# One row of a partition moved from the tail pieces into the first load of a streaming ReLU-mean kernel (127 to 126 rows a partition)

## The chip, the cores and the metric

The kernel runs on one core of a Trainium2 chip. The metric is the device time of one execution in microseconds (us). An execution's span, as the profile draws it, is some 1.3 us shorter than its time.

## The reference

```
batch, seq, dim = 32, 512, 1024
x: float32 [32, 512, 1024]
return mean(maximum(x, 0), axis=-1)      # float32 [32, 512]
```

It is 16,384 rows of 4 KiB, 67.1 MB to be read once, and 64 KiB to be written.

## The kernel before

The rows are dealt to the 128 partitions. The first 128 rows (one block) go one to a partition, in a load of its own; the other 16,256 rows are cut into 128 runs of 127 consecutive rows, one run to a partition. Of these 127, 7 x 16 come in full tiles of 16 rows (8 MiB a load, 64 KiB without a break in each partition) through three buffers, then pieces of 7, 4, 2 and 1 rows, then the last row in column pieces of 512, 256 and 256.

```
    xfirst, xmain = xf[:P, :], xf[P:, :]
    ...
    J = J - 1
    xr = xmain.rearrange("(p j) d -> p j d", p=P, j=J)
    ...
    row_pieces = [7, 4, 2, 1]
    ...
    def buf_free(t):
        if t >= BUFS:
            nc.sync.wait_ge(act, t - BUFS + 1)
            nc.sync.wait_ge(dve, t - BUFS + 1)

    for t in range(full):
        buf_free(t)
        if t == 0:
            load(-1, row0[:, :], xfirst)
        load(t, bufs[t % BUFS][:, :, :], xr[:, t * NB:(t + 1) * NB, :])
        ...                      # (t == BUFS: store of the first block's means)
```

ScalarE (ACT) takes the even rows, with a Relu that accumulates along the row, VectorE (DVE) the odd ones, with max and add. The first block's means stand one to a partition; a 32x32 transpose brings them into four rows of 32, which are stored with four packets. The very last column piece is DVE's; one store of all the other means ends the kernel. The first two loads (the block and tile 0) are issued ahead of the barrier at the kernel's entry.

## Time and profile before

| | before |
|---|---|
| time, median | 161.34 us (161.31 to 161.44, 3 runs) |
| span of the profile | 160.2 us |
| DVE / ACT busy | 46% / 44% |
| packets of the DMA engines, share of 16 engines' span | 97.7% |
| tile 0 computed from / tile 6 from | 22.98 / 139.30 us |

Read it so: with the queue filled nearly all the time and both engines half idle, the time is the time of the transfers, plus what stands ahead of the first packet and what stands behind the last one. A change can matter in three ways only: in how long the bytes take in packets of their size, at the start, and at the end. The lines themselves are in the prediction below.

### The profile page before, as it was taken

The page shows a single profiled execution, that of the slowest core. Times are in us where ns is not written, and L with a number is a line of the kernel's source. Part 1 is how long each engine was busy: PE and PEld are TensorE (multiplying, and loading weights), DVE is VectorE, ACT ScalarE, POOL GpSimd, SP SyncE. Part 2 cuts the span into 40 slices and gives each one's busy share as a digit, 9 for nine tenths or more (in the row PEclk, how much of TensorE's full clock was granted, in tenths as well). Part 3 has the DMA queues.
Part 4 walks back from the last instruction along what each step waited for, and adds up shares of the span by engine and source line. Part 5 has one row for each costly group of instructions (what it writes and reads, how often), then busy time and mean ns, then how long its engine had stood idle before and what let it go on. Part 6 is the DMA issues. An engine that isn't in the chain of part 4 may idle for free. (4 is left out here: it accounts for less than half of the span.)

```text
span 160.2 us, 347 instructions
## 1 busy us (share of the span) xinstructions
DVE 73.3 (46%) x131; ACT 70.4 (44%) x133; POOL 1.3 (1%) x9
## 2 busy tenths in 40 slices
DVE  0000029900498006960079500993009920299984
ACT  1400029800496006950079300991009900299983
POOL 1000000000000000000000000000000000000001
DMA  9969969979989899699699699699699797998992
GB/s 393 507 278 523 507 278 523 442 344 523 409 376 523 360 425 524 294 491 523 262 524 523 262 523 524 262 523 523 262 524 458 327 523 327 425 451 367 419 412 102
DMA packets 2312, 67.18 MB, mean 419 GB/s; under 512 B 392, under 2 KB 648, under 8 KB 1032
## 3 DMA queue, kind: packets, MB, share of 16 engines
q1 hardware_dynamic: 2312, 67.18, 97.7%
HBM read 67.11 MB, written 0.07 MB: 419 GB/s over the span
## 5 line engine op out<-in xcount | busy, mean ns | idle before, releaser
L20 DVE TENSOR_SCALAR_CACHE_REDUCE rows<-rows 128x1024 f32<-128x1024 f32 (+1 forms) x63 | 72.1, 1208 | 78.9 <-DMA rows<-in_x_dram 78.7
L15 ACT ACTIVATE rows<-rows 128x1024 f32<-128x1024 f32 x64 | 66.2, 1035 | 84.1 <-DMA rows<-in_x_dram 83.9
L15 ACT ACTIVATION_READ_ACCUMULATOR rows<-rows 128x1 f32 x64 | 11.9, 186 | 0.0
L20 DVE DVE_READ_ACCUMULATOR rows<-rows 128x1 f32 x63 | 5.2, 82 | 0.0
L168 DVE STREAM_TRANSPOSE turned<-mean 128x32 f32<-128x32 f32 x1 | 0.2, 213 | 5.9 <-ACT row L164 5.9
L164 ACT ACT_TABLE_LOAD x1 | 1.3, 1283 | 3.3 <-DMA row<-in_x_dram 3.3
L157 POOL TENSOR_SCALAR res<-sums 128x112 f32<-128x112 f32 (+1 forms) x2 | 0.5, 250 | 154.0 <-DVE rows L20 154.0
L164 ACT ACTIVATE row<-row 128x1024 f32<-128x1024 f32 x1 | 1.1, 1056 | 0.0
L15 ACT ACTIVATE last<-last 128x512 f32<-128x512 f32 x1 | 0.6, 630 | 0.0
L20 DVE TENSOR_SCALAR_CACHE_REDUCE last<-last 128x256 f32<-128x256 f32 x1 | 0.4, 420 | 0.3 <-DMA last<-in_x_dram 0.3
L197 DVE SCALAR_TENSOR_TENSOR last<-last,scale 128x258 f32<-128x258 f32 x1 | 0.4, 428 | 0.1
L142 POOL MEMSET scale<- 128x258 f32 x1 | 0.3, 314 | 0.0
L187 POOL TENSOR_SCALAR res<-part 128x1 f32<-128x1 f32 x1 | 0.3, 267 | 0.6 <-DVE rows L20 0.6
L164 ACT ACTIVATION_READ_ACCUMULATOR row<-row 128x1 f32 x1 | 0.2, 186 | 0.0
L15 ACT ACTIVATION_READ_ACCUMULATOR last<-last 128x1 f32 x1 | 0.2, 186 | 0.0
L141 POOL MEMSET mean<- 128x32 f32 x1 | 0.1, 126 | 1.5 <-POOLq L55 1.5
L232 POOL MEMSET const-uint8-127<- 128x1 uint8 x1 | 0.1, 103 | 0.0
L232 POOL MEMSET const-bfloat16-1.0<- 128x1 bf16 x1 | 0.1, 102 | 0.0
L232 POOL MEMSET const-float32-0.0<- 128x1 f32 x1 | 0.1, 99 | 0.2 <-issue 0.2
L232 POOL MEMSET const-float32-1.0<- 128x1 f32 x1 | 0.1, 99 | 0.0
L20 DVE DVE_READ_ACCUMULATOR last<-last 128x1 f32 x1 | 0.1, 83 | 0.0
L197 DVE DVE_READ_ACCUMULATOR last<-last,scale 128x1 f32 x1 | 0.1, 82 | 0.0
## 6 DMA issues: line engine op xcount, KB each, us to landing
rows<-in_x_dram SPq DMA_DIRECT2D x1, 3584.0 KB, 38.1
rows<-in_x_dram SPq DMA_DIRECT2D x1, 2048.0 KB, 42.6
rows<-in_x_dram SPq DMA_DIRECT2D x1, 1024.0 KB, 44.7
row<-in_x_dram SPq DMA_DIRECT2D x1, 512.0 KB, 3.3
rows<-in_x_dram SPq DMA_DIRECT2D x1, 512.0 KB, 45.4
last<-in_x_dram SPq DMA_DIRECT2D x1, 256.0 KB, 45.6
last<-in_x_dram SPq DMA_DIRECT2D x2, 128.0 KB, 45.4
rows<-in_x_dram SPq DMA_DIRECT2D x7, 48.8
```

The source lines that it names most:

```text
L15: return nc.scalar.activation(out=src, in_=src, func=ACT.Relu, accum_out=acc)
L20: return nc.vector.tensor_scalar(out=src, in0=src, scalar1=0.0, scalar2=init, op0=ALU.max, op1=ALU.add, accum_out=acc,)
L141: nc.gpsimd.memset(mean0[:, :], 0.0)
L142: nc.gpsimd.memset(scale[:, :], inv).then_inc(pool, 1)
L157: nc.gpsimd.tensor_scalar(out=res[:, lo:hi], in0=sums[:, lo:hi], scalar1=inv, scalar2=0.0, op0=ALU.mult, op1=ALU.add,)
L164: nc.scalar.activation(out=row0[:, :], in_=row0[:, :], func=ACT.Relu, scale=inv, accum_out=mean0[:, 0:1],).then_inc(first, 1)
L168: nc.vector.transpose(turned0[:, :], mean0[:, :]).then_inc(first, 1)
L187: nc.gpsimd.tensor_scalar(out=res[:, J - 2:J - 1], in0=part[:, 0:1], scalar1=part[:, 1:2], scalar2=inv, op0=ALU.add, op1=ALU.mult,).then_i ...
L197: nc.vector.scalar_tensor_tensor(out=last[:, 768:], in0=last[:, 768:], scalar=0.0, in1=scale[:, :], op0=ALU.max, op1=ALU.mult, accum_out=r ...
L232: nc = _bacc.Bacc("TRN2", target_bir_lowering=False, num_devices=1)
```

## The change

126 rows a partition instead of 127. The first two blocks of 128 rows, not only the first, come one row of each to a partition, in one load ahead of the full tiles; in exchange the first tail piece has 6 rows instead of 7. The intent may be read as taking a row from the end of the stream, where computing and loading meet, and giving it to the start, where the computing engines have nothing to do.

```
--- before.py
+++ after.py
@@ -62,9 +62,9 @@
     J = R // P
     inv = 1.0 / D
 
-    xfirst, xmain = xf[:P, :], xf[P:, :]
-    outfirst, outmain = out.flatten()[:P], out.flatten()[P:]
-    J = J - 1
+    xfirst, xmain = xf[:2 * P, :].rearrange("(c p) d -> p c d", c=2), xf[2 * P:, :]
+    outfirst, outmain = out.flatten()[:2 * P], out.flatten()[2 * P:]
+    J = J - 2
     xr = xmain.rearrange("(p j) d -> p j d", p=P, j=J)
     outr = outmain.rearrange("(p j) -> p j", p=P, j=J)
 
@@ -72,7 +72,7 @@
     BUFS = 3
     full = J // NB
 
-    row_pieces = [7, 4, 2, 1]
+    row_pieces = [6, 4, 2, 1]
     assert full * NB + sum(row_pieces) + 1 == J
     col_pieces = [512, 256, 256]
     assert sum(col_pieces) == D
@@ -87,7 +87,7 @@
     last = sbuf("last", P, D + 2)
     scale = sbuf("scale", P, D // 4 + 2)
 
-    row0, mean0, turned0 = sbuf("row0", P, D), sbuf("mean0", P, 32), sbuf("turned0", P, 32)
+    row0, mean0, turned0 = sbuf("row0", P, 2, D), sbuf("mean0", P, 32), sbuf("turned0", P, 32)
 
 
     loaded = [nc.alloc_semaphore(f"loaded{i}") for i in range(full + len(row_pieces) + len(col_pieces) + 1)]
@@ -117,14 +117,15 @@
     for t in range(full):
         buf_free(t)
         if t == 0:
-            load(-1, row0[:, :], xfirst)
+            load(-1, row0[:, :, :], xfirst)
         load(t, bufs[t % BUFS][:, :, :], xr[:, t * NB:(t + 1) * NB, :])
         if t == BUFS:
 
             nc.sync.wait_ge(first, 2)
-            nc.sync.dma_start(
-                out=outfirst.rearrange("(q i) -> q i", i=32), in_=turned0[0:P:32, :],
-            ).then_inc(stored, 16)
+            for c in range(2):
+                nc.sync.dma_start(
+                    out=outfirst[c * P:(c + 1) * P].rearrange("(q i) -> q i", i=32), in_=turned0[c:P:32, :],
+                ).then_inc(stored, 16)
     j0 = full * NB
     buf_free(full)
     xt = bufs[full % BUFS]
@@ -161,9 +162,11 @@
     nc.scalar.wait_ge(pool, 1)
     nc.vector.wait_ge(pool, 1)
     nc.scalar.wait_ge(loaded[-1], 16)
-    nc.scalar.activation(
-        out=row0[:, :], in_=row0[:, :], func=ACT.Relu, scale=inv, accum_out=mean0[:, 0:1],
-    ).then_inc(first, 1)
+    for c in range(2):
+        done = nc.scalar.activation(
+            out=row0[:, c, :], in_=row0[:, c, :], func=ACT.Relu, scale=inv, accum_out=mean0[:, c:c + 1],
+        )
+    done.then_inc(first, 1)
     nc.vector.wait_ge(first, 1)
     nc.vector.transpose(turned0[:, :], mean0[:, :]).then_inc(first, 1)
     for t in range(full):
@@ -207,7 +210,7 @@
     used = [s.num for s in (*loaded, act, dve, pool, first)]
     assert used == list(range(used[0], used[0] + len(used)))
     nc.sync.sem_clear(range(used[0], used[-1] + 1))
-    nc.sync.wait_ge(stored, 32).then_inc(stored, -32)
+    nc.sync.wait_ge(stored, 48).then_inc(stored, -48)
 
     for e, hint in zip(hinted, hints):
         e.br_lt(flag, 1, on_true="rows_begin", on_false="rows_end").branch_hint(hint)
```

More of the change, by code (lines that the diff above doesn't have):

```diff
@@ L63 @@
     inv = 1.0 / D
-    xfirst, xmain = xf[:P, :], xf[P:, :]
-    outfirst, outmain = out.flatten()[:P], out.flatten()[P:]
-    J = J - 1
+    xfirst, xmain = xf[:2 * P, :].rearrange("(c p) d -> p c d", c=2), xf[2 * P:, :]
+    outfirst, outmain = out.flatten()[:2 * P], out.flatten()[2 * P:]
+    J = J - 2
     xr = xmain.rearrange("(p j) d -> p j d", p=P, j=J)
@@ L73 @@
     full = J // NB
-    row_pieces = [7, 4, 2, 1]
+    row_pieces = [6, 4, 2, 1]
     assert full * NB + sum(row_pieces) + 1 == J
@@ L88 @@
     scale = sbuf("scale", P, D // 4 + 2)
-    row0, mean0, turned0 = sbuf("row0", P, D), sbuf("mean0", P, 32), sbuf("turned0", P, 32)
+    row0, mean0, turned0 = sbuf("row0", P, 2, D), sbuf("mean0", P, 32), sbuf("turned0", P, 32)
     loaded = [nc.alloc_semaphore(f"loaded{i}") for i in range(full + len(row_pieces) + len(col_pieces) + 1)]
@@ L119 @@
         if t == 0:
-            load(-1, row0[:, :], xfirst)
+            load(-1, row0[:, :, :], xfirst)
         load(t, bufs[t % BUFS][:, :, :], xr[:, t * NB:(t + 1) * NB, :])
@@ L124 @@
             nc.sync.wait_ge(first, 2)
-            nc.sync.dma_start(
-                out=outfirst.rearrange("(q i) -> q i", i=32), in_=turned0[0:P:32, :],
-            ).then_inc(stored, 16)
+            for c in range(2):
+                nc.sync.dma_start(
+                    out=outfirst[c * P:(c + 1) * P].rearrange("(q i) -> q i", i=32), in_=turned0[c:P:32, :],
+                ).then_inc(stored, 16)
     j0 = full * NB
@@ L163 @@
     nc.scalar.wait_ge(loaded[-1], 16)
-    nc.scalar.activation(
-        out=row0[:, :], in_=row0[:, :], func=ACT.Relu, scale=inv, accum_out=mean0[:, 0:1],
-    ).then_inc(first, 1)
+    for c in range(2):
+        done = nc.scalar.activation(
+            out=row0[:, c, :], in_=row0[:, c, :], func=ACT.Relu, scale=inv, accum_out=mean0[:, c:c + 1],
+        )
+    done.then_inc(first, 1)
     nc.vector.wait_ge(first, 1)
@@ L209 @@
     nc.sync.sem_clear(range(used[0], used[-1] + 1))
-    nc.sync.wait_ge(stored, 32).then_inc(stored, -32)
+    nc.sync.wait_ge(stored, 48).then_inc(stored, -48)
     for e, hint in zip(hinted, hints):
```

## The prediction

> **What bounds the kernel now.** I read the page first, then the waits of the compute engines, the waits of the issuing queue, and last the timeline around the first full tile and around the end. The page gives the balance:
>
> ```profile
> span 160.2 us, 347 instructions
> DVE 73.3 (46%) x131; ACT 70.4 (44%) x133; POOL 1.3 (1%) x9
> ...
> DMA packets 2312, 67.18 MB, mean 419 GB/s; under 512 B 392, under 2 KB 648, under 8 KB 1032
> ...
> q1 hardware_dynamic: 2312, 67.18, 97.7%
> ```
>
> The two computing engines work less than half of the span; the packets fill 97.7% of the time that 16 DMA engines have. So the transfers are the bound. The view of waits says what the engines wait for in the rest of their time, and the waits of the issuing queue say whether the loads are issued early enough:
>
> ```profile
> ACT rows L15 <- DMA rows<-in_x_dram: 83.9, 9, 17.2
> DVE rows L20 <- DMA rows<-in_x_dram: 78.7, 8, 16.9
> ...
> SPq L115 <- DVE rows L20: 104.6, 5, 29.5
> ```
>
> (us in total, times, longest.) ACT and DVE wait for rows alone. The queue waits for DVE to free a buffer, but that wait costs nothing: the page's list of issues has 48.8 us from issue to landing as the median of the full 16-row loads, and one tile takes 19.4 us (next paragraph), so a load stands some two and a half tiles deep in the queue and the 16 engines never run dry.
>
> The timeline gives the rate. Columns are start, duration, engine, line, operation; the bracket is the idle time before:
>
> ```profile
> 22.98 1.22 DVE L20 TENSOR_SCALAR_CACHE_REDUCE rows<-rows 128x1024 f32<-128x1024 f32 x1 [16.86 <-DMA rows<-in_x_dram]
> ...
> 139.30 1.22 DVE L20 TENSOR_SCALAR_CACHE_REDUCE rows<-rows 128x1024 f32<-128x1024 f32 x1 [10.29 <-DMA rows<-in_x_dram]
> ...
> 147.82 1.06 ACT L15 ACTIVATE rows<-rows 128x1024 f32<-128x1024 f32 x1
> 148.42 1.22 DVE L20 TENSOR_SCALAR_CACHE_REDUCE rows<-rows 128x1024 f32<-128x1024 f32 x1
> ...
> 152.71 1.22 DVE L20 TENSOR_SCALAR_CACHE_REDUCE rows<-rows 128x1024 f32<-128x1024 f32 x1 [0.79 <-DMA rows<-in_x_dram]
> ...
> 155.20 1.22 DVE L20 TENSOR_SCALAR_CACHE_REDUCE rows<-rows 128x1024 f32<-128x1024 f32 x1
> ...
> 156.49 0.75 DVE L20 TENSOR_SCALAR_CACHE_REDUCE rows<-rows 128x576 f32<-128x576 f32 x1
> ...
> 157.54 0.42 DVE L20 TENSOR_SCALAR_CACHE_REDUCE last<-last 128x256 f32<-128x256 f32 x1 [0.29 <-DMA last<-in_x_dram]
> ...
> 158.06 0.43 DVE L197 SCALAR_TENSOR_TENSOR last<-last,scale 128x258 f32<-128x258 f32 x1
> ...
> 158.57 0.35 SPq L205 DMA_DIRECT2D out_dram<-res  x1
> ```
>
> Tile 0 of the full tiles has landed at 22.98 and tile 6 at 139.30: six tiles in 116.32 us, 19.39 us for each. That is 8,388,608 bytes in 19.39 us, 432.7 GB/s. The tail pieces then arrive one after the other, each computed nearly as it lands; the last column piece has landed just before 158.06, and the store closes the span 1.6 us after its issue.
>
> **What the Trainium skill says.** "DMA: Bandwidth & Descriptors", section "Where 436 GB/s comes from", gives 16 ports x 32 B x 850 MHz = 435.2 GB/s. The trace agrees: 432.7 GB/s measured is 99.4% of it. So the part of the kernel that decides cannot run noticeably faster in any layout. The same page, section "Latency and other measured facts", has an entry on HBM row pitch at large powers of two: copies with 512 KiB between partitions made 207 GB/s against 214 at full rate, and 4 MiB halved it; adding 4 KiB restored it. The pitch of the kernel before is 127 x 4 KiB = 508 KiB, and no slowing is seen in its trace; that of the change is 126 x 4 KiB = 504 KiB, which no run shows yet. Third, the page's section "Anatomy of one DMA" says that the fixed cost of a load doesn't grow with its size. The trace is in line with it: the first load, 0.5 MB, took 3.3 us to land, of which its packets, as worked out below, fill about 1.8.
>
> **The change part by part.** Every byte is still read once, so only the cost of the bytes by packet size, and their order, changes. The trace's records of single packets have their durations (8 of each load to each of the 16 engines, back to back): 4,096-byte packets take 159 ns, 16,384-byte ones 611, 28,672-byte ones 1,062, 65,536-byte ones 2,418.
>
> - *Added at the front:* one more row to each partition in the first load, 8 more 4 KiB packets per engine: 8 x 0.159 = 1.27 us. As a check, the single-row piece at the end took 156.49 - 155.20 = 1.29 us. Those packets stand in the queue ahead of all the tiles, so all full tiles land 1.27 us later: tile 0 at 24.25, tile 6 at 140.57.
> - *Removed at the back:* the piece of 7 rows becomes one of 6. From 611 ns for 16 KiB to 1,062 for 28 KiB is 150 ns per 4 KiB, so 24 KiB takes about 912 ns, and 8 x (1.062 - 0.912) = 1.20 us go. (147.82 - 139.30 = 8.52 us for the whole piece confirms 8 x 1.062.)
> - *Net of the transfers:* +0.07 us. One row per partition moves from large packets, where it costs 1.20, to small ones, where it costs 1.27.
> - *One more ACTIVATE and accumulator read* on ACT (about 1.04 us, from the cadence of the ACT rows) ahead of the transpose: at about 7 us, when ACT would then idle until 24. Off the path. In return ACT has one row fewer in the first tail piece (three instead of four).
> - *One more store of 512 B:* the four packets of the existing one took 13 ns each; the queue issues it in about 0.63 us, as the first, at 33 us, when its next load isn't to be issued before 51.6. Off the path, about 0.01 us of transfer at most. The final wait for 48 instead of 32 looks at semaphores that rose long before.
> - *First issue:* 256 pieces instead of 128 are to be described. The present first issue takes 389 ns, and the issue from the queue to the first packet lies open at the start. I allow 0 to 0.15 us, 0.03 in the middle; this is a judgement, no row has it.
> - *The tail of DVE:* it is not shorter although a row went, since the removed row (even) was ACT's. DVE starts tile 6 1.27 us later, but the pieces behind it land only 0.07 later. Eight rows at its cadence of 1.14 us (148.42 - 139.30 = 9.12) take it from 140.57 to 149.69; three more rows to 153.11, where the 4-row piece has been there since 152.78 (152.71 + 0.07); two rows to 155.39 (the 2-row piece landed 155.27); one row to 156.53, where the next piece lands at 156.56. So DVE, 0.3 us behind, has just caught up there. Even 0.2 us more would vanish in the 0.29 us idle before 157.54. Nothing is added at the end.
>
> Sum: 161.34 + 0.07 + 0.01 + 0.03 = 161.45 us.
>
> **The rivals.** *A: the pitch matters.* A pitch of 504 KiB may spread the 128 streams over the memory worse than 508 KiB (steps from one partition to the next of -8 KiB modulo 512 KiB instead of -4 KiB, so only 64 distinct places modulo 512 KiB instead of 128). Then each 64 KiB packet would be longer: if the skill's 207 against 214 applied here, 3% of 7 x 19.4 us is about 4.4 us, for a time near 166. Against it: the lowest of the packets, 2,415 ns, is already the limit of the DMA engine, the memory need not give more than 433 GB/s, and the skill's 4 KiB of padding sufficed where 8 KiB is used here. *B: the pitch helps.* The mean of the 64 KiB packets is 2,430 ns against a lowest of 2,415: over 56 packets per engine 0.84 us are all that a better spread could win, 160.6 at best. I expect a random part of that. *C: DVE doesn't catch up.* If the rows were slower or the piece came earlier, DVE would be late by some 0.3 us at the last piece, of which 0.29 is absorbed; worst about 161.7. *D: the smaller work on ACT at the tail pays.* ACT waits for rows already before 152.71 (0.62 us idle), so it wins nothing.
>
> **Range and chances.** Runs of before lie within 0.13 us. The named terms move the time between -0.2 (part of B) and +0.3 (a slower first issue, C); A is an unlikely jump. So 161.45 us, 161.15 to 161.8 eight times in ten. Faster by over 2% would need 158.2 or less, below what the limit of the engines leaves: 0.01. Slower by over 2% needs A nearly in full: 0.03. Within 2%: 0.96.
>
> **What would show each step right or wrong.** In the profile of the change tile 0 should start at about 24.25 instead of 22.98; tile 6 at 140.57; the 4-row piece at 153.1 on DVE without an idle gap, where before it waited 0.79 us; the last piece at about 158.13 instead of 158.06. The mean distance of two full tiles should stay 19.39 us: a larger one is rival A, a smaller one B. If tile 0 comes later than 24.4, the first issue was mis-sized. If the gap before the last column pieces is gone and the end is late, it is C. The prediction is wrong if the time leaves 161.15 to 161.8.

## The result, and the profile after

| | before | after |
|---|---|---|
| time, median, all runs beside one another | 161.44 us (161.31 to 161.70, 6 runs) | 161.55 us (161.45 to 161.65, 6 runs) |
| ratio | | 1.0004, 95% interval 0.9991 to 1.0017 |
| time of the profiled execution | 161.59 us | 161.45 us |
| span of the profile | 160.2 us | 160.1 us |

A ratio, here and below, is the mean time of one kernel's runs over that of the other's of the same rounds, so it is not quite the ratio of the medians that are quoted.

The page of the profile after, with the balance of the engines and of the queue:

```profile
span 160.1 us, 348 instructions
...
DVE 73.0 (46%) x131; ACT 70.3 (44%) x133; POOL 1.3 (1%) x9
...
DMA packets 2448, 67.18 MB, mean 420 GB/s; under 512 B 400, under 2 KB 656, under 8 KB 1168
...
q1 hardware_dynamic: 2448, 67.18, 97.8%
```

There are 136 packets more (2,448 - 2,312), all of them under 8 KB: 128 of 4 KiB for the second block, and 8 under 512 B, which come with the second small store (four of 128 B and four semaphore writes in the records of packets). All else stands: the same bytes, the same bound.

The timeline of the profile after (start us, duration us, engine, line, operation, operands; in brackets the idle time before it and what ended it):

```profile
24.23 1.22 DVE L20 TENSOR_SCALAR_CACHE_REDUCE rows<-rows 128x1024 f32<-128x1024 f32 x1 [15.51 <-DMA rows<-in_x_dram]
...
140.34 1.22 DVE L20 TENSOR_SCALAR_CACHE_REDUCE rows<-rows 128x1024 f32<-128x1024 f32 x1 [10.14 <-DMA rows<-in_x_dram]
...
152.52 1.06 ACT L15 ACTIVATE rows<-rows 128x1024 f32<-128x1024 f32 x1 [0.64 <-DMA rows<-in_x_dram]
...
152.88 1.22 DVE L20 TENSOR_SCALAR_CACHE_REDUCE rows<-rows 128x1024 f32<-128x1024 f32 x1
...
155.16 1.22 DVE L20 TENSOR_SCALAR_CACHE_REDUCE rows<-rows 128x1024 f32<-128x1024 f32 x1
...
156.30 0.75 DVE L20 TENSOR_SCALAR_CACHE_REDUCE rows<-rows 128x576 f32<-128x576 f32 x1
...
157.36 0.42 DVE L20 TENSOR_SCALAR_CACHE_REDUCE last<-last 128x256 f32<-128x256 f32 x1 [0.29 <-DMA last<-in_x_dram]
...
157.88 0.43 DVE L200 SCALAR_TENSOR_TENSOR last<-last,scale 128x258 f32<-128x258 f32 x1
...
158.39 0.35 SPq L208 DMA_DIRECT2D out_dram<-res  x1
```

Three things are to be seen. Tile 0 comes 1.25 us later than before (24.23 against 22.98). Tile 6 comes only 1.04 us later (140.34 against 139.30): the six tiles between took 116.11 us, 19.35 each, where they took 116.32, 19.39 each, in the trace before. And DVE has no idle time before 152.88, where before it waited 0.79 us: the piece was there at 152.52, when ACT took it up, but DVE was still at work. It has caught up by 156.30, when both engines start the last whole row; the pause of 0.29 us before the column piece is what it was.

So two small departures from the prediction want an explanation: the smoother stream of tiles in this one trace (0.2 us), and a measured time that is not lower for it. Both are far below 2%; the experiments tell a part of what they come from.

### The profile page after: what moved, and what is told of

It is laid out like the page before. It is cut to its first block, busy times and chain, and to the rows that moved or that the text cites. A ratio compares the mean times of both kernels' runs of the same rounds, so it can differ in the third digit from the quotient of the medians.

```text
span 160.1 us, 348 instructions
## 1 busy us (share of the span) xinstructions
DVE 73.0 (46%) x131; ACT 70.3 (44%) x133; POOL 1.3 (1%) x9
## 2 busy tenths in 40 slices
DMA packets 2448, 67.18 MB, mean 420 GB/s; under 512 B 400, under 2 KB 656, under 8 KB 1168
## 3 DMA queue, kind: packets, MB, share of 16 engines
q1 hardware_dynamic: 2448, 67.18, 97.8%
## 5 line engine op out<-in xcount | busy, mean ns | idle before, releaser
L15 ACT ACTIVATE rows<-rows 128x1024 f32<-128x1024 f32 (+1 forms) x63 | 65.1, 1035 | 82.5 <-DMA rows<-in_x_dram 82.4
L166 ACT ACTIVATE row<-row 128x1024 f32<-128x1024 f32 x2 | 2.1, 1048 | 0.0
```

The costliest lines, as they stand in the source:

```text
L15: return nc.scalar.activation(out=src, in_=src, func=ACT.Relu, accum_out=acc)
L166: done = nc.scalar.activation(out=row0[:, c, :], in_=row0[:, c, :], func=ACT.Relu, scale=inv, accum_out=mean0[:, c:c + 1],)
```

## The experiments

The theory: the transfers are the bound at any of these layouts; a row moved from the tail to the front costs the difference of 4 KiB packets against large ones, takes 1.2 us from the time in which DVE catches up, and nothing else of the change is on the path. The rivals: the pitch of the partitions (126 rows instead of 127) slows or smooths the stream; packet size costs nothing in a full queue; DVE's catching up never binds; the issue of the first load matters. There were twelve runs, in three groups, each group beside the kernel before on one chip. Every result was right except in the two runs where it is said. The edits below show changed lines alone; unchanged lines are left out, between changed ones too.

### Both kernels once more

No edit. First the kernel before:

> The kernel before, unchanged, run beside itself. All theories: ratio 1.000 within 0.1%, 161.3 to 161.7 us. What it is for: a second trace of the same program. If the mean distance of two full tiles, 19.387 us in the first trace, comes out near 19.35 here too (as in the trace of the change), the 0.23 us that the change won over the six tiles is scatter; if it stays at 19.38 to 19.40, it may be the pitch (rival B).

Then the change:

> The change, unchanged, with five rounds for a narrower interval. My theory (one row moved from large packets to 4 KiB ones, nothing else on the path): ratio 1.0005, 161.5 us, tile 0 landed about 1.25 us later than before, mean tile distance as in the other null run within 0.03 us. Rival B (the pitch of 126 rows helps): tile distance again 0.03 us shorter than before, which wins back 0.2 us, ratio 0.9995 or less.

Measured: the kernel before 161.34 us (161.24 to 161.57, 5 runs), ratio to its own twin 0.9995 (0.9982 to 1.0008). The change 161.54 us (161.38 to 162.24, 6 runs), ratio 1.0019 (1.0000 to 1.0037). The timelines, tile 0 and tile 6, first of the kernel before:

```profile
23.00 1.22 DVE L20 TENSOR_SCALAR_CACHE_REDUCE rows<-rows 128x1024 f32<-128x1024 f32 x1 [16.90 <-DMA rows<-in_x_dram]
...
139.38 1.22 DVE L20 TENSOR_SCALAR_CACHE_REDUCE rows<-rows 128x1024 f32<-128x1024 f32 x1 [10.17 <-DMA rows<-in_x_dram]
```

and of the change:

```profile
24.43 1.22 DVE L20 TENSOR_SCALAR_CACHE_REDUCE rows<-rows 128x1024 f32<-128x1024 f32 x1 [15.50 <-DMA rows<-in_x_dram]
...
140.56 1.22 DVE L20 TENSOR_SCALAR_CACHE_REDUCE rows<-rows 128x1024 f32<-128x1024 f32 x1 [10.14 <-DMA rows<-in_x_dram]
```

Six tiles take 116.38 us (19.40 each) in the one and 116.13 (19.36 each) in the other, as in the first pair of traces. The 0.2 us is thus in both pairs of traces. Whether it is in the other executions too is not shown, and there is a reason for doubt: the executions of the kernel before whose traces were kept took 161.59 and 161.57 us, 0.2 over the median of its runs (161.34 both times), while those of the change, 161.45 and 161.60, lie within 0.1 us of its medians (161.55 and 161.54). The front of the change is later this time: tile 0 by 1.43 us instead of 1.25. My expectation that the tile distances would be alike within 0.03 us was missed by 0.01; the times are those of the theory, or 0.1 us over, and not those that rival B asked for (a ratio of 0.9995 or less).

### The pitch and the number of blocks, apart

128 rows to the run of a partition, so 512 KiB from one partition to the next; the first load takes row 127 of each run:

```
-    xfirst, xmain = xf[:P, :], xf[P:, :]
-    outfirst, outmain = out.flatten()[:P], out.flatten()[P:]
+    xr = xf.rearrange("(p j) d -> p j d", p=P, j=J)
+    outr = out.flatten().rearrange("(p j) -> p j", p=P, j=J)
-    xr = xmain.rearrange("(p j) d -> p j d", p=P, j=J)
-    outr = outmain.rearrange("(p j) -> p j", p=P, j=J)
+    xfirst = xr[:, J, :]
-    sums, res, part = sbuf("sums", P, J), sbuf("res", P, J), sbuf("part", P, 2)
+    sums, res, part = sbuf("sums", P, J), sbuf("res", P, J + 1), sbuf("part", P, 2)
-        if t == BUFS:
-
-            nc.sync.wait_ge(first, 2)
-            nc.sync.dma_start(
-                out=outfirst.rearrange("(q i) -> q i", i=32), in_=turned0[0:P:32, :],
-            ).then_inc(stored, 16)
-        out=row0[:, :], in_=row0[:, :], func=ACT.Relu, scale=inv, accum_out=mean0[:, 0:1],
+        out=row0[:, :], in_=row0[:, :], func=ACT.Relu, scale=inv, accum_out=res[:, J:J + 1],
-    nc.vector.wait_ge(first, 1)
-    nc.vector.transpose(turned0[:, :], mean0[:, :]).then_inc(first, 1)
+    nc.sync.wait_ge(first, 1)
-    nc.sync.wait_ge(stored, 32).then_inc(stored, -32)
+    nc.sync.wait_ge(stored, 16).then_inc(stored, -16)
```

> 128 rows a partition, 512 KiB from partition to partition; the first load takes row 127 of each partition in place of a block of its own; the transpose and its store are gone. The result is right. My theory (the DMA engines are the limit, the pitch does nothing here): 64 KiB packets as before, tile distance 19.35 to 19.40 us, time 161.2 to 161.6, ratio 0.999 to 1.001. Rival A (the pitch matters[...]): tile distance near 20.0 us, time near 166, ratio 1.03.

Measured: 161.81 us (161.46 to 161.94, 4 runs), ratio 1.0021 (1.0007 to 1.0036).

```profile
23.24 1.22 DVE L20 TENSOR_SCALAR_CACHE_REDUCE rows<-rows 128x1024 f32<-128x1024 f32 x1 [23.24 <-DMA rows<-in_x_dram]
...
139.63 1.22 DVE L20 TENSOR_SCALAR_CACHE_REDUCE rows<-rows 128x1024 f32<-128x1024 f32 x1 [10.31 <-DMA rows<-in_x_dram]
```

The tiles are 116.39 / 6 = 19.40 us apart by these lines, and 19.42 by the records of landings (DVE's first instruction starts 0.14 us after the landing here and 0.03 in the kernel before; it is the first of all on DVE here, which may be why), against 19.39 in the kernel before, so even the power-of-two pitch slows the stream by 0.03 us a tile at most. Rival A asked for 20.0 us and a time near 166; it falls. The time came out 0.2 us over what I expected, and I don't know from which part: tile 0 lands 0.15 us later here (23.10 against 22.95 in the records of landings), and the first load now reads rows 512 KiB apart.

Next, the pitch of 126 rows with all else as before, and the pitch of 127 rows with all else as in the change. Both results are wrong, since some rows are read twice and others not at all.

```
-    xr = xmain.rearrange("(p j) d -> p j d", p=P, j=J)
+    xr = xmain[:P * (J - 1), :].rearrange("(p j) d -> p j d", p=P, j=J - 1)
-        load(i, last[:, c:c + w], xr[:, J - 1, c:c + w])
+        load(i, last[:, c:c + w], xr[:, J - 2, c:c + w])
```

> The kernel before in all its instructions and sizes (one block of 128 rows ahead, 127 rows a partition), but the rows of a partition start every 126 rows, so neighbours share a row; the result is wrong on purpose. Both traces of before have a mean tile distance of 19.39 us, every trace with two or more blocks ahead 19.35. If the pitch of 126 rows is what makes the stream smooth (rival B), the tile distance is 19.35 here, the 64 KiB packets have a mean of 2,421 ns instead of 2,430, and the time is 0.2 us below before, ratio 0.999. If it is the longer first load that does it, 19.39 as in before, ratio 1.000. Tile 0 lands at 22.95 in both.

```
-    xr = xmain.rearrange("(p j) d -> p j d", p=P, j=J)
+    xr = xf[P:, :].rearrange("(p j) d -> p j d", p=P, j=J + 1)
```

> The change in all its instructions and sizes (two blocks ahead, 126 rows a partition), but the rows of a partition start every 127 rows; the result is wrong on purpose. The counterpart of the run with the pitch of 126 rows and one block. If the pitch makes the stream smooth, the tile distance is 19.39 here and the time 0.2 us over the change, 161.75, ratio 1.002 to 1.003; if the longer first load does it, 19.35, and the time is that of the change, 161.55, ratio 1.001. Tile 0 lands at 24.2 to 24.4 in both.

Measured: with the pitch of 126 and one block 161.62 us (161.28 to 162.25, 6 runs), ratio 1.0021 (1.0001 to 1.0040); with the pitch of 127 and two blocks 161.78 us (161.76 to 161.86, 5 runs), ratio 1.0020 (1.0007 to 1.0033). The timeline of the former, then of the latter:

```profile
22.88 1.22 DVE L20 TENSOR_SCALAR_CACHE_REDUCE rows<-rows 128x1024 f32<-128x1024 f32 x1 [16.71 <-DMA rows<-in_x_dram]
...
139.14 1.22 DVE L20 TENSOR_SCALAR_CACHE_REDUCE rows<-rows 128x1024 f32<-128x1024 f32 x1 [10.15 <-DMA rows<-in_x_dram]
```

```profile
24.52 1.22 DVE L20 TENSOR_SCALAR_CACHE_REDUCE rows<-rows 128x1024 f32<-128x1024 f32 x1 [15.50 <-DMA rows<-in_x_dram]
...
140.64 1.22 DVE L20 TENSOR_SCALAR_CACHE_REDUCE rows<-rows 128x1024 f32<-128x1024 f32 x1 [10.15 <-DMA rows<-in_x_dram]
```

One block at the pitch of 126: 116.26 us, 19.38 a tile, with one distance of 19.50 us among them by the records of landings. Two blocks at the pitch of 127: 116.12 us, 19.35 a tile, and none over 19.36. So the smoother stream goes with the second block ahead and not with the pitch; rival B had seen an effect that is in the traces, and named the wrong cause for it. The records of single packets agree: the mean of the 64 KiB packets is 2,430, 2,432, 2,427 and 2,433 ns in the four traces with one block ahead and full tiles all through (the pitches of 127, 127 again, 126 and 128 rows), and 2,421 or 2,420 in every trace with two to four blocks in one load. What differs are single long packets all along the stream: of those that start later than 12 us, 46, 40, 19 and 60 take over 2,480 ns in the former, and 0 to 5 in the latter. The times don't follow so neatly: those of the former scatter more than any others here, and that of the latter is the one that the pitch theory had given, though its tiles are smooth; its tile 0 is the latest of the two-block kernels with one load (24.52 us), which would account for it. The second block as such isn't needed either: the next run has one block ahead, but two tiles in 4 KiB packets, and its stream is as smooth behind them. Why more small packets ahead go with a calmer stream, no run shows.

### Packet size alone

Tiles 0 and 1 of the kernel before take the even and the odd ones of the first 32 rows, so that they come in 4 KiB packets; the rest stands.

```
-        load(t, bufs[t % BUFS][:, :, :], xr[:, t * NB:(t + 1) * NB, :])
+        rows_of = slice(t, 2 * NB, 2) if t < 2 else slice(t * NB, (t + 1) * NB)
+        load(t, bufs[t % BUFS][:, :, :], xr[:, rows_of, :])
-            j = j0 + k
-            done = (dve_row if j % 2 else act_row)(nc, xt[:, k, :], sums[:, j:j + 1])
+            e = j0 + k
+            j = 2 * k + i if i < 2 else e
+            done = (dve_row if e % 2 else act_row)(nc, xt[:, k, :], sums[:, j:j + 1])
-                done.then_inc(dve if j % 2 else act, 1)
+                done.then_inc(dve if e % 2 else act, 1)
```

> The kernel before, but tile 0 takes the even and tile 1 the odd ones of the first 32 rows of a partition, so these two tiles come in 4 KiB packets instead of 64 KiB ones; pitch, order of the bytes and tail stay. The result is right. My theory (a row costs 8 x 0.159 = 1.27 us in 4 KiB packets and 8 x 2.418 / 16 = 1.21 in 64 KiB ones, and all of it stands on the path): 32 rows x 0.063 = 2.0 us more, 163.5 us, ratio 1.0125; tile 0 lands 1.0 us later, tile 1 to 6 2.0 us later. Rival (the packet size costs nothing in the steady stream, the durations of single packets overlap): 161.5, ratio 1.000.

Measured: 163.63 us (163.60 to 163.70, 4 runs), ratio 1.0139 (1.0125 to 1.0154). The timeline, first tile 1 of the kernel before, from its first trace:

```profile
42.32 1.22 DVE L20 TENSOR_SCALAR_CACHE_REDUCE rows<-rows 128x1024 f32<-128x1024 f32 x1 [10.14 <-DMA rows<-in_x_dram]
```

and tiles 0, 1 and 6 of this run:

```profile
24.01 1.22 DVE L20 TENSOR_SCALAR_CACHE_REDUCE rows<-rows 128x1024 f32<-128x1024 f32 x1 [17.75 <-DMA rows<-in_x_dram]
...
44.48 1.22 DVE L20 TENSOR_SCALAR_CACHE_REDUCE rows<-rows 128x1024 f32<-128x1024 f32 x1 [11.26 <-DMA rows<-in_x_dram]
...
141.24 1.22 DVE L20 TENSOR_SCALAR_CACHE_REDUCE rows<-rows 128x1024 f32<-128x1024 f32 x1 [10.14 <-DMA rows<-in_x_dram]
```

Tile 0 is 1.03 us later than before (24.01 - 22.98), and tile 1 2.16 us later (44.48 against 42.32): 2.16 / 32 = 0.068 us a row, where 0.063 had been worked out. It is all on the path, and the median rises by as much, 163.63 - 161.41 = 2.22 us, over that of the kernel before in the same rounds. The rival, for which small packets cost nothing in a full queue, falls. Behind tile 1 the stream is smooth here too: the five distances from tile 1 to tile 6 take 96.76 us, 19.35 each, and no 64 KiB packet takes over 2,480 ns. So tile 6 is only 1.94 us later than in the trace before (141.24 against 139.30), although the median rose by 2.22. This speaks for a stream of the kernel before that is smooth in its usual executions and rough in the two traced ones; it doesn't prove it.

### More blocks ahead

Three blocks ahead, then four. There isn't room for them in a buffer of their own, so they use the third tile's buffer before that tile does. The edit against the change, for four:

```
-    xfirst, xmain = xf[:2 * P, :].rearrange("(c p) d -> p c d", c=2), xf[2 * P:, :]
-    outfirst, outmain = out.flatten()[:2 * P], out.flatten()[2 * P:]
-    J = J - 2
+    xfirst, xmain = xf[:4 * P, :].rearrange("(c p) d -> p c d", c=4), xf[4 * P:, :]
+    outfirst, outmain = out.flatten()[:4 * P], out.flatten()[4 * P:]
+    J = J - 4
-    row_pieces = [6, 4, 2, 1]
+    row_pieces = [4, 4, 2, 1]
-    row0, mean0, turned0 = sbuf("row0", P, 2, D), sbuf("mean0", P, 32), sbuf("turned0", P, 32)
+    row0, mean0, turned0 = bufs[2][:, :4, :], sbuf("mean0", P, 32), sbuf("turned0", P, 32)
+        if t == 2:
+            nc.sync.wait_ge(first, 1)
-            for c in range(2):
+            for c in range(4):
-    for c in range(2):
+    for c in range(4):
-    nc.sync.wait_ge(stored, 48).then_inc(stored, -48)
+    nc.sync.wait_ge(stored, 80).then_inc(stored, -80)
```

(For three: 3 in place of 4, tail pieces of 5, 4, 2, 1, a last wait for 64.)

> The change taken one step further: three blocks of 128 rows ahead (into the third full tile's buffer, for want of room; the load of that tile waits for ACT to be done with them, at some 13 us), 125 rows a partition, a first tail piece of 5. The result is right. My theory: each row moved to the front costs 0.07 us of transfer and takes 1.2 us from the time that DVE has to catch up after tile 6. From the trace of the change: tile 6 at 140.34 + 1.27 = 141.61; DVE is then through its eight rows, two, two and one at 156.43, when the last piece landed at 156.34, so it is 0.1 us late there and on time again at the last column pieces: ratio to before 1.001 to 1.002, 161.6 us. Rival (the catching up of DVE is never the bound, only transfers count): the same, so this run tells the two apart only by the missing idle of DVE before the last piece.

> Four blocks ahead, 124 rows a partition, first tail piece of 4. The result is right. My theory: tile 6 at 140.34 + 2.54 = 142.88; DVE through its eight rows at 152.00, two more at 154.28, two more at 156.56, one at 157.70, its part of the last row at 158.46, the column piece, and the closing instruction at 158.98, where it is at 157.88 in the change: 1.1 us later, ratio to before about 1.0075, 162.6 us. Rival (only transfers count, DVE always has slack): 2 x 0.07 us over the change, 161.7 us, ratio 1.002.

And four blocks with DVE relieved at the last whole row:

```
-    act_row(nc, prev[:, :448], part[:, 0:1]).then_inc(act, 1)
+    act_row(nc, prev[:, :896], part[:, 0:1]).then_inc(act, 1)
-    dve_row(nc, prev[:, 448:], part[:, 1:2]).then_inc(dve, 1)
+    dve_row(nc, prev[:, 896:], part[:, 1:2]).then_inc(dve, 1)
```

> As blocks4, but of the last whole row ACT takes 896 columns and DVE 128 (448 and 576 before). The result is right. My theory (DVE's lateness is the cause in blocks4): DVE is at the column piece some 0.5 us earlier, ACT then ends with its own piece at about 158.3, and the closing instruction starts at about 158.4, 0.6 us before that of blocks4; ratio to before about 1.004, 162.1 us. If the time of blocks4 comes from transfers or from the wait ahead of the third tile, this run is as slow as blocks4.

Measured: three blocks 162.14 us (161.85 to 162.40, 4 runs), ratio 1.0049 (1.0028 to 1.0069); four 162.91 us (162.85 to 162.97, 4 runs), ratio 1.0092 (1.0075 to 1.0109); four with ACT's larger share 162.35 us (162.25 to 162.55, 4 runs), ratio 1.0059 (1.0040 to 1.0077). The timeline of DVE at the end, four blocks:

```profile
158.18 0.75 DVE L20 TENSOR_SCALAR_CACHE_REDUCE rows<-rows 128x576 f32<-128x576 f32 x1
...
158.85 0.41 DVE L20 TENSOR_SCALAR_CACHE_REDUCE last<-last 128x256 f32<-128x256 f32 x1
...
159.37 0.43 DVE L202 SCALAR_TENSOR_TENSOR last<-last,scale 128x258 f32<-128x258 f32 x1
```

and with the larger share for ACT:

```profile
158.34 0.41 DVE L20 TENSOR_SCALAR_CACHE_REDUCE last<-last 128x256 f32<-128x256 f32 x1
...
158.85 0.43 DVE L202 SCALAR_TENSOR_TENSOR last<-last,scale 128x258 f32<-128x258 f32 x1
```

With four blocks the pause of 0.29 us before the column piece is gone: DVE runs straight through to the closing instruction, which starts at 159.37, 1.1 us after the last byte has landed at 158.25 (before: 158.06 and 157.82). Giving 448 of DVE's columns to ACT brings the closing instruction forward by 0.52 us and the median by 0.56. So DVE's lateness is what bounds the end of the four blocks. The change, with two, stands two steps short of it: with three, DVE still has a pause of 0.25 us before the column piece.

Three blocks were 0.5 us slower than expected all the same, and that isn't DVE. Tile 0 of the change and its extensions starts at 24.23 and 24.43, 25.75, and 27.25 us: a further row in the first load costs some 1.4 to 1.5 us there, not the 1.27 of its packets. The records of packets show where it goes: the 4 KiB packets of the first load are slow at the very start (up to 656 ns in the first trace of before, 938 in that of the change), and summed up they fill 1.61 and 1.45 us per engine in the two traces of before, where 8 x 0.159 would be 1.27, and 3.14 and 3.00 in the two of the change, where 16 x 0.159 would be 2.54. That is 0.2 to 0.3 us over the steady duration for one row and 0.5 to 0.6 for two (0.3 in the traces of the pitch of 127 with two blocks and of one load with three issued ahead, 2.82 and 2.81). With three blocks it is 4.57 instead of 3.82. That covers about half of the miss: tile 0 is 0.25 us later than 24.23 + 1.27. The rest shows in no trace, since the run with the profile was the fastest of its four (161.85). In the four blocks, too, tile 6 came 0.48 us later than worked out (143.36 for 142.88), and the closing instruction 0.39 (159.37 for 158.98).

### One load or two

The change with its two blocks in two loads instead of one, all three first loads ahead of the barrier:

```
-            load(-1, row0[:, :, :], xfirst)
+            for c in range(2):
+                load(-1, row0[:, c, :], xfirst[:, c, :])
-    nc.scalar.wait_ge(loaded[-1], 16)
+    nc.scalar.wait_ge(loaded[-1], 32)
-    issue_ahead_of_entry_barrier(nc, 2)
+    issue_ahead_of_entry_barrier(nc, 3)
```

> The change, but its two first blocks come in two loads of 128 rows, one after the other, in place of one; all three first loads are issued ahead of the entry barrier. The result is right. My theory (the issue of the first load is a small term: the same packets of 4 KiB follow each other in the queue, and the first of them starts at 1.03 to 1.1 us either way): as the change within 0.1 us, 161.5, tile 0 at 24.2 to 24.4 us. Rival (describing 256 pieces in one issue delays the start): tile 0 some 0.1 us earlier than in the change, and the time by as much.

Measured: 162.61 us (162.53 to 162.82, 4 runs), ratio 1.0071 (1.0054 to 1.0087). Both theories missed: I had taken this part of the change, "in one load", for nothing. Two more runs take the edit apart. In the first, the two loads stay but tile 0 is issued after the barrier:

```
-    issue_ahead_of_entry_barrier(nc, 3)
+    issue_ahead_of_entry_barrier(nc, 2)
```

> The run with two loads of one block came out 1.1 us slower than the change, with tile 0 at 25.23 instead of 24.2 to 24.4. It differs in two things: two loads for one, and three loads ahead of the entry barrier for two. Here the two blocks come in two loads still, but only they are issued ahead of the barrier, and tile 0 after it. If the third issue ahead of the barrier is at fault, the time is that of the change, 161.5, and tile 0 lands at 24.4. If a further boundary between two loads is, the time stays near 162.6.

In the second, the change itself has a third load ahead of the barrier:

```
-    issue_ahead_of_entry_barrier(nc, 2)
+    issue_ahead_of_entry_barrier(nc, 3)
```

> The change with one thing altered: the load of tile 1 too is issued ahead of the entry barrier, so three loads are. The result is right. Counterpart of the run before it: if the third issue ahead of the barrier costs the time, about 162.5 us, tile 0 landed 0.8 us late; if a further boundary between two loads does, 161.5 as the change, tile 0 at 24.2 to 24.4.

Measured: two loads with two issued ahead 162.19 us (161.82 to 162.46, 4 runs), ratio 1.0044 (1.0028 to 1.0059); one load with three issued ahead 161.67 us (161.60 to 161.82, 4 runs), ratio 1.0016 (1.0001 to 1.0030). The start of tile 0 in the timelines of the two loads, of the two loads with two ahead, and of the one load with three ahead, in this order:

```profile
25.25 1.22 DVE L20 TENSOR_SCALAR_CACHE_REDUCE rows<-rows 128x1024 f32<-128x1024 f32 x1 [16.77 <-DMA rows<-in_x_dram]
```

```profile
24.80 1.22 DVE L20 TENSOR_SCALAR_CACHE_REDUCE rows<-rows 128x1024 f32<-128x1024 f32 x1 [16.36 <-DMA rows<-in_x_dram]
```

```profile
24.28 1.22 DVE L20 TENSOR_SCALAR_CACHE_REDUCE rows<-rows 128x1024 f32<-128x1024 f32 x1 [15.46 <-DMA rows<-in_x_dram]
```

A third issue ahead of the barrier does no harm by itself. Two loads do: some 0.6 us of time with tile 0 behind the barrier, and 1.1 with it ahead. The view by windows shows the loss; its columns are the stretch in us, its length, busy time of DVE, ACT and POOL with counts, the clock, the DMA share and GB/s. A packet counts whole in one window, so single windows can exceed the pace of the engines; up to 8 us the bytes of the two are the same. Then the two loads:

```profile
8.00:10.00 2.00, 0.21 (x1) 0.16 (x2) 0.00 (x0) 1.00 0.92 393
```

and the change:

```profile
8.00:10.00 2.00, 0.21 (x1) 0.39 (x2) 0.00 (x0) 1.00 1.21 524
```

In this window the two loads are (524 - 393) GB/s x 2 us = 262 KB short: four packets of 64 KiB start after 10.00 us instead of before it, so four of the engines are late. How late they are the view doesn't say: with two issued ahead the same window has 524 GB/s, as in the change. The landings of the 16 engines, from the trace's semaphore records, do say it, and also that it is never made good (us from the start of the span; earliest, twelfth, thirteenth and last engine):

```
                          tile 0                          last column piece
two loads                 23.88  24.39  24.88  25.23      157.41  157.84  158.29  158.62
two loads, two ahead      23.72  23.93  24.29  24.77      157.22  157.40  157.72  158.16
the change                23.88  24.12  24.13  24.20      157.38  157.62  157.63  157.67
```

Four engines come late out of the start, and 133 us later four are late still, by nearly as much (the records don't name the engine, so that they are the same four is inferred). In the two loads the earliest landings of tile 0 and of the last piece are 133.5 us apart and the last ones 133.4, so all engines keep the same pace, and the start of the slowest one sets the end. The records of packets show where the four fall behind: of tile 0, the first sixteen 64 KiB packets, one to an engine, take 2,418 or 2,419 ns in the first trace of the change and have all ended by 6.89 us. With two loads and two ahead, twelve have ended by 6.68 us and four, which take 2,915 to 3,099 ns, between 7.03 and 7.54. With two loads and three ahead, twelve have ended by 7.18 us and four between 7.65 and 8.00: one of these takes 3,720 ns, and three start late, at 4.77 to 5.10 us. Why these packets take longer there, no run shows, and it stays open.

## Why the prediction was right

The prediction was 161.45 us and no change; measured were 161.55 and no change. The shift of 0.11 us was met to 0.01 (161.34 to 161.45 said, 161.44 to 161.55 measured), but that is in part luck: in the traces two terms are off in opposite directions (the front up to 0.2 us later than said, the stream 0.2 us shorter), and the interval of the ratio, 0.9991 to 1.0017, is wider than the shift. Term by term:

- **The bound.** Right. In every run the time follows the landings of the loads, except in the four-block runs, made to let DVE bind.
- **The net of the transfers, +0.07 us.** The term held for the stream: 0.068 us a row by the interleaved tiles, and 24 KiB packets of 912 ns in the trace of the change, as interpolated. At the very start it was too small, since the packets there take longer than the 159 ns of the steady stream: the front row costs about 1.25 to 1.5 us where 1.27 was said (tile 0 of the change starts 1.25 and 1.43 us later in the two pairs of traces). The prediction's sign for this, tile 0 later than 24.4, came in the second trace (24.43); it had put it down to the first issue, but the first packet starts only 0.07 us later there (1.10 for 1.03).
- **The distance of two tiles.** Said to stay at 19.39 us; it fell to 19.35, 0.2 us over six tiles. This hid the first deviation in the profiles: span 160.2 and 160.2 before, 160.1 and 160.3 after; the closing instruction starts 0.18 us earlier than before in the first pair (157.88 for 158.06) and 0.01 later in the second, where 0.07 later was said. By its size it was rival B's effect, at a quarter of its largest size (0.2 of 0.84 us), but not by the pitch: it stays with two blocks at the old pitch and goes with one block at the new one.
- **Rival A, the pitch as a brake.** Given a small chance, and rightly: 504, 508 and 512 KiB with one block ahead give 19.38, 19.39 and 19.40, and 19.42 us a tile.
- **The tail of DVE.** Right in its steps: 153.11 was said for DVE's first row of the 4-row piece and 152.88 measured, which is 0.23 early as is tile 6 (140.34 for 140.57); no idle time before it; caught up when the last whole row is there. Rival C, DVE not catching up, comes true two rows further on, in the four blocks. Rival D, that ACT's smaller share pays, was put aside rightly: ACT still waits for the 4-row piece, 0.64 us where it waited 0.62.
- **The extra ACTIVATE and the extra store.** Off the path, as said; the transpose runs at 8.50 us, and DVE then waits 15.51 us for tile 0.
- **The first issue.** It takes 0.45 us instead of 0.39, and the first packet starts at 1.08 instead of 1.03 us: 0.05, where 0.03 stood in the sum.

What stays open: whether the two kernels' streams differ in their usual executions at all. If they don't, the cost of the front row shows in full. That would fit the times: the change is 0.1 us slower in the medians and equal in the spans of the profiles, the traced executions of the kernel before are 0.2 us slower than its median, and the interleaved tiles cost 2.22 us in the medians and 1.94 in the traces. Against it, the traces of the other two kernels with one block ahead are rough too, and their executions are not slow ones: 161.45 us at the pitch of 126 (median 161.62) and 161.79 at that of 128 (161.81).

## What to carry to other kernels

In a load-bound stream like this one a row costs the duration of its packets wherever it stands (somewhat more in the first microseconds), so moving rows between the ends of the stream is worth little more than the difference in packet size; look at what catches up behind the last full tile before taking rows from there, because after a large tile the computing engines are behind the loads, and need the time in which the small pieces come to catch up. Put small first rows into one load rather than two, and measure it: here an engine that came late out of the first microseconds stayed late to the end. And compare the time of a traced execution with the median of its kernel before explaining a few tenths of a microsecond from its trace.

## What the Trainium skill lacked or had wrong

- "DMA: Bandwidth & Descriptors", section "Latency and other measured facts", on HBM row pitch: it gives 207 against 214 GB/s for copies at 512 KiB. Loads of 64 KiB runs into 128 partitions on one core show no slowing of that size (3% would be 0.6 us a tile): the tile distance is 19.42 us at 512 KiB against 19.39 and 19.40 at 508 KiB. The page's copies were between two HBM tensors.
- Same page, section "Why small descriptors are slow (HBM only)": a fixed overhead of some 3 cycles a packet would be, as an estimate from the page's 850 MHz, 3.5 ns for a 4 KiB packet. In the stream a row costs 159 ns in 4 KiB packets and 2,418 / 16 = 151 in 64 KiB ones, 8 ns more (the section's second term, 32 bytes of metadata, would add 1.2 ns at the 27.1 bytes a ns of a 64 KiB packet here); and no page says that the first packets of a kernel take up to 656 or 938 ns.
- Same page, section "Rules for kernel authors": "Coalesce into one large transfer; under 64 KB you're paying mostly overhead" is given for many small transfers, as a matter of overhead. No page tells that a second small load ahead of a large one can hold up single engines for good: 0.6 to 1.1 us here, for 0.5 MB more in a load of its own instead of the same load.
- No page says that the mean 64 KiB packet of the long stream goes with how it was started: 2,427 to 2,433 ns in the traces with one block ahead, 2,420 or 2,421 with two to four blocks in one load, 2,422 behind two tiles in 4 KiB packets.
